# ScalarE empties more banks of the gate recurrence, and one load of y is spread over output products

## The chip, the cores and the metric

The kernel runs on one core of a Trainium2 chip. The metric is the device time of one execution in microseconds (us), as the median of several runs. Times inside an execution come from one profiled execution, read by the hardware profiler; its span is counted from the first to the last instruction. TensorE (PE) multiplies matrices, VectorE (DVE) does elementwise work and scans, ScalarE (ACT) applies functions and copies, GpSimd (POOL) takes some elementwise work, and SyncE (SP) issues the DMA transfers.

## What the kernel computes

Two layers of a diffusion backbone over 1024 latent tokens and 256 context tokens, width 1024, all in float32. Both layers begin with an RMSNorm whose result is shifted and scaled by vectors made from a conditioning input ("modulation"), and end with a gated residual add. Layer 0 has two branches beside each other. Branch A is a gated linear recurrence (RG-LRU): eight heads of 128 channels, a short convolution, two sigmoid gates, and a scan in both directions. Branch B is windowed attention with 16 heads. Layer 1 is another linear recurrence, in chunks (HGRN2). Cut to what the change touches:

```
u      = rmsnorm(h) * w * (1 + scale) + shift        # shift, scale, gate from silu(c) @ ada_w + ada_b
xa, ga, gb = u @ w_in[...]                            # branch A's input, the gates of A and of B
r, i   = sigmoid(conv(xa) @ wa + ba), sigmoid(conv(xa) @ wx + bx)
a      = exp(-8 * r * softplus(-lam));  b = sqrt(1 - a*a) * i * conv(xa)
ya     = scan(a, b) forward + scan(a, b) backward
h      = h + gate * (concat(ya * silu(ga), yb * silu(gb)) @ w_out)      # silu(g) = g * sigmoid(g)
```

## The kernel before, in words

Channels lie on the 128 partitions and tokens on the free axis; the 1280 tokens are three chunks, 0 and 1 of 512 latent tokens and 2 of the 256 context tokens. A float32 product is made of three products of a faster format, from a high and a low half of each operand, so one tile of 512 columns is 3 x 8 matmuls into one bank of PSUM. The weights' halves are made on the chip: `load_w` (L83) loads a block, ScalarE casts it (L93), GpSimd or VectorE takes the difference (L94).

The loop of branch A (L402 to L475) runs over j = 0 to 7, one head each. In iteration j TensorE makes: the gate product of branch A (three chunks, L417 to L422: ScalarE writes the sigmoid from the bank into `sga`, VectorE multiplies it by the bank, which empties the bank); the projection X of the next iteration (copied out by ScalarE, L398); the recurrence's two gates R and I in both directions (twelve products, L436); for j >= 2 the gate product of branch B (three chunks, L466 to L472, into `sgb`, in the same manner, stored in DRAM at L473); and one group of modulation vectors (L163), whose result goes through a ScalarE copy (L166) and a transpose (L174) into a bank that VectorE adds a bias to (L176, `ada_fin`) in the next iteration. ScalarE, GpSimd and VectorE make the recurrence's coefficients between (L437 to L447), VectorE scans (L449 to L456), adds the directions (L460, L461), multiplies them into `sga` (L462, L463), and `sga` is stored (L464).

Banks of PSUM in this stage: four with the tag "mm" for the products, three "gate" for R and I, and one "ada" that the product and the transpose of modulation share. In SBUF, `sga` and `sgb` share one tag of two buffers, so a new one can be written only when the store of an earlier one has landed.

The order of the instructions on each engine is fixed when the kernel is built. In this loop a planner makes it: it takes, engine by engine, what is ready by its own estimates, the earliest in program order first. `tc.high_priority(offset=n)` puts instructions as if they stood n instructions earlier in the program; PRI_E is 100, PRI_W 300. At run time every engine works through its list in order.

After attention, the second half of the output projection (`out_B`, L771) adds branch B's share: `load_yB` (L786) loads y of a chunk in eight pieces `yr` (three buffers), ScalarE casts each to the high half and GpSimd or VectorE makes the low half (L690 to L693). `acc` of each chunk holds the residual and branch A's share, loaded from DRAM (L774); for each of eight blocks m TensorE makes the product of a chunk into one of two banks "mmo", and VectorE adds it to `acc` (L780), ScalarE and VectorE form the sum of squares for the next norm. The first call takes the chunks 2 and 0, the second chunk 1.

Of the kernel before, what the change touches and what calls it, by code (L numbers as in the profile page):

```python
# [11 lines left out]
F32 = mybir.dt.float32  # L12
F32R = mybir.dt.float32r
U8 = mybir.dt.uint8
AF = mybir.ActivationFunctionType
ALU = mybir.AluOpType
# [33 lines left out]
def backbone_kernel(ctx: ExitStack, tc: tile.TileContext, a: dict, out):  # L50
# [82 lines left out]
    def drain(*gens):  # L133
        for g in gens:
            for _ in g:
                pass
# [15 lines left out]
    mods = ctile([128, 2, 6, 4, 2], "mods")  # L152
# [16 lines left out]
    def ada_mod(wpool, psp, l, g, bufs=NADA):  # L169
        ada_fin(psp, ada_mm(wpool, psp, l, g, bufs), l, g)  # L170

    def ada_fin(psp, row, l, g):
        pc = psp.tile([128, 512], F32, tag="ada", name="ps_c", bufs=1)
        PE.transpose(pc[:, :128], row, ident)  # L174
        with tc.high_priority(offset=PRI_E):
            V.tensor_tensor(out=mods[:, l, g], in0=pc[:, :128].rearrange("p (b x) -> p b x", x=32)[:, :, 0:2],  # L176
                            in1=adab[:, l, g].unsqueeze(2).to_broadcast([128, 4, 2]), op=ALU.add)
            if g < 4:
                V.scalar_tensor_tensor(out=amul[:, l, 2 * g:2 * g + 2], in0=mods[:, l, g, 2:4], scalar=1.0,
                                       in1=normw[:, l * 8 + 2 * g:l * 8 + 2 * g + 2].unsqueeze(2)  # L180
                                       .to_broadcast([128, 2, 2]), op0=ALU.add, op1=ALU.mult)
# [110 lines left out]
    def gemm_block(w, c, psp, tag="mm", bufs=4):  # L292
        n = CHUNKS[c][1]
        ps = psp.tile([128, 512], F32, tag=tag, name="mm", bufs=bufs)
        mm3(ps[:, :n], gemm_terms(w, c))
        return ps[:, :n]
# [105 lines left out]
    for j in range(8):  # L402
        X = X_next
        gw = load_w(a["rgw"][j], 512, "gw", rg, bufs=(1, 1))
        uc = rg.tile([128, W], F32, tag="uc", name="uc")
        V.tensor_scalar(out=uc, in0=X[:, 0:W], scalar1=convw[:, j * 4:j * 4 + 1],
                        scalar2=convb[:, j:j + 1], op0=ALU.mult, op1=ALU.add)
        for k in range(1, 4):
            V.scalar_tensor_tensor(out=uc, in0=X[:, k:k + W], scalar=convw[:, j * 4 + k:j * 4 + k + 1],
                                   in1=uc, op0=ALU.mult, op1=ALU.add)  # L410
        uh = rg.tile([128, W], F32R, tag="uh", name="uh")
        ul = rg.tile([128, W], F32R, tag="ul", name="ul")
        V.tensor_copy(uh, uc)
        V.tensor_tensor(out=ul, in0=uc, in1=uh.bitcast(F32), op=ALU.subtract)
        sga = rg.tile([128, T], F32, tag="sga", name="sga", bufs=2)
        w = load_w(a["w0"][8 + j]) if j else w_first[1]
        for c in (2, 0, 1):  # L417
            o, n = CHUNKS[c]
            ps = gemm_block(w, c, psA) if j else ps_first[1, c]
            with tc.high_priority(offset=PRI_E):  # L420
                S.activation(sga[:, o:o + n], ps, AF.Sigmoid)
                V.tensor_tensor(out=sga[:, o:o + n], in0=sga[:, o:o + n], in1=ps, op=ALU.mult)  # L422
        if j < 7:
            X_next = x_proj(j + 1)
        if j:
            ada_fin(psA, row, *ada_lg)
        R, I, A, M = ([rg.tile([128, W], F32, tag=t_, name=t_, bufs=2) for _ in range(2)] for t_ in "RIAM")

        for d in range(2):
            for g_, dst in ((1, R[d]), (0, I[d])):  # L430
                m = (d * 2 + g_) * 128
                for o, n in ((0, 512), (512, 512), (1024, 260)):
                    ps = psA.tile([128, 512], F32, tag="gate", name="gate", bufs=3)
                    mm3(ps[:, :n], [(gw[0][:, m:m + 128], gw[1][:, m:m + 128],
                                     uh[:, o:o + n], ul[:, o:o + n])])
                    S.activation(dst[:, o:o + n], ps[:, :n], AF.Sigmoid, bias=rgb[:, g_, d, j:j + 1])  # L436
            last = S.activation(M[d], R[d], AF.Tanh, scale=sneg[:, d, j:j + 1]).ins  # L437
            G.tensor_tensor(out=I[d], in0=I[d], in1=uc, op=ALU.mult)
        with tc.issue_after(last), tc.high_priority(offset=0):
            for d in range(2):  # L440
                S.activation(A[d], R[d], AF.Exp, scale=spos[:, d, j:j + 1])
        for d in range(2):
            S.activation(R[d], A[d], AF.Square)
            V.scalar_tensor_tensor(out=R[d], in0=R[d], scalar=1.0, in1=M[d], op0=ALU.add, op1=ALU.mult)
        for d in range(2):
            S.activation(R[d], R[d], AF.Sqrt, bias=tiny_c)
            V.tensor_tensor(out=I[d], in0=I[d], in1=R[d], op=ALU.mult)  # L447
            if d == 0:
                V.tensor_tensor_scan(out=M[d][:, CTX0:W], data0=A[d][:, CTX0:W], data1=I[d][:, CTX0:W],  # L449
                                     initial=0.0, op0=ALU.mult, op1=ALU.add)  # L450
                V.tensor_tensor_scan(out=M[d][:, 0:NL], data0=A[d][:, 0:NL], data1=I[d][:, 0:NL],
                                     initial=M[d][:, W - 1:W], op0=ALU.mult, op1=ALU.add)
            else:
                V.tensor_tensor_scan(out=M[d][:, CTX0:W][:, ::-1], data0=A[d][:, CTX0:W][:, ::-1],
                                     data1=I[d][:, CTX0:W][:, ::-1], initial=0.0, op0=ALU.mult, op1=ALU.add)
                V.tensor_tensor_scan(out=M[d][:, 0:NL][:, ::-1], data0=A[d][:, 0:NL][:, ::-1],  # L456
                                     data1=I[d][:, 0:NL][:, ::-1], initial=M[d][:, CTX0:CTX0 + 1],
                                     op0=ALU.mult, op1=ALU.add)
        yf, yb_ = M
        V.tensor_tensor(out=yf[:, 0:NL], in0=yf[:, 0:NL], in1=yb_[:, 0:NL], op=ALU.add)  # L460
        V.tensor_tensor(out=yf[:, CTX0:W], in0=yf[:, CTX0:W], in1=yb_[:, CTX0:W], op=ALU.add)  # L461
        V.tensor_tensor(out=sga[:, 0:NL], in0=sga[:, 0:NL], in1=yf[:, 0:NL], op=ALU.mult)  # L462
        V.tensor_tensor(out=sga[:, NL:T], in0=sga[:, NL:T], in1=yf[:, CTX0:W], op=ALU.mult)  # L463
        SY.dma_start(ya_d[j], sga)  # L464
        if j >= 8 - NGB:
            w = load_w(a["w0"][18 + NGB + j])  # L466
            sg = rg.tile([128, T], F32, tag="sga", name="sgb", bufs=2)
            for c, (o, n) in enumerate(CHUNKS):
                ps = gemm_block(w, c, psA)
                with tc.high_priority(offset=PRI_E):  # L470
                    S.activation(sg[:, o:o + n], ps, AF.Sigmoid)
                    V.tensor_tensor(out=sg[:, o:o + n], in0=sg[:, o:o + n], in1=ps, op=ALU.mult)  # L472
            SY.dma_start(gb_d[(j + NGB - 8) // 2][:, j % 2], sg)  # L473
        ada_lg = (0, 4 + j) if j < 2 else (1, j - 2)
        row = ada_mm(rg, psA, *ada_lg)  # L475
# [213 lines left out]
    def split_y(yp, src, n, hi, lo, k):  # L689
        yr = yp.tile([128, n], F32, tag="yr", name="yr", bufs=3, padded_shape=[128, 512])  # L690
        SY.dma_start(yr, src)
        S.copy(hi[:, k], yr)
        (V if k % 2 else G).tensor_tensor(out=lo[:, k], in0=yr, in1=hi[:, k].bitcast(F32), op=ALU.subtract)  # L693
# [74 lines left out]
    hp0, hp0_st = open_pool("hp0")  # L768
    acc, n1ss = {}, {}

    def out_B(cs, yB, npool, psp, tag, bufs):  # L771
        for c in cs:
            acc[c] = npool.tile([128, 8, CHUNKS[c][1]], F32, tag=f"acc{c}", name=f"acc{c}")
            SY.dma_start(acc[c], hA_d[c])  # L774
            n1ss[c] = npool.tile([128, CHUNKS[c][1]], F32, tag=f"n1ss{c}", name="n1ss")
        for m in range(8):
            w = load_w(a["wo0"][8 + m], split=cs == (1,))
            for c in cs:
                ps, gt = out_half(w, m, yB[c], c, psp, tag, bufs)
                V.scalar_tensor_tensor(out=acc[c][:, m], in0=ps, scalar=gt, in1=acc[c][:, m],  # L780
                                       op0=ALU.mult, op1=ALU.add)
                if c < 2:
                    SY.dma_start(h1_d[:, m, c * 512:c * 512 + 512], acc[c][:, m])
                sumsq(npool, n1ss[c], acc[c][:, m], m)

    def load_yB(c):  # L786
        yB[c] = new_y(c)
        for k in range(8):
            split_y(yrp, yb_d[k // 2][c][:, k % 2], CHUNKS[c][1], *yB[c], k)

    yB = {}
    load_yB(2)
    load_yB(0)
    load_yB(1)
    out_B((2, 0), yB, hp0, psB, "mmo", 2)
    psB_st.close()
    psC, psC_st = open_pool("psC", space=PSUM)
    hp, hp_st = open_pool("hp", side="right")
# [425 lines left out]
```

## Time and profile before

| | |
|---|---|
| median of 3 runs | 1988.04 us (1984.24 to 1995.71) |
| the profiled execution | 1988.59 us |
| its span | 1986.7 us |
| TensorE busy | 1886.1 us (95%), mean granted clock 0.984 |
| VectorE, ScalarE, GpSimd busy | 1146.0, 956.1, 475.1 us |
| DMA | 207.53 MB |

Busy is the time in which an engine worked on at least one instruction; it is not on its own what bounds the kernel. The granted clock is the share of TensorE's full clock that the chip allowed. In the rows further down, L12 is line 12 of the kernel, "a<-b,c" is the written tile and the ones read, and the bracket at the end of a row gives the idle time of the engine before the instruction and what ended it.

### The profile page before, as it was taken

The numbers are of one execution on the slowest core, as the hardware profiler recorded it, in microseconds if no ns is written. First come the engines' busy times: TensorE is split into PE (matmuls) and PEld (weight loads), VectorE is DVE, ScalarE is ACT, GpSimd is POOL, SyncE is SP. The second block draws the span as 40 slices with busy tenths as digits, with TensorE's granted clock in tenths as the row PEclk, the third lists the DMA queues.
The fourth block names the chain that finished last, engine by engine and source line by source line (L and its number), as shares of the span: only waits on it lengthen the run. The fifth ranks groups of instructions, "written<-read, shape, count | busy, mean of one in ns | idle before, by whom it ended". The sixth has DMA issues, their size and how long they took to land. (4 is left out here: it accounts for less than half of the span.)

```text
span 1986.7 us, 36590 instructions
## 1 busy us (share of the span) xinstructions
PE 1886.1 (95%) x15228; PEld 1605.0 (81%) x15228; DVE 1146.0 (58%) x1920; ACT 956.1 (48%) x1766; POOL 475.1 (24%) x309
## 2 busy tenths in 40 slices
PE   6989999999999999999989999999999999998987
PEld 5878888889888787887768889898888779777676
DVE  3766555564465556556534756564746664565656
ACT  4478666682156578556532443434324433343332
POOL 0133332320111024213232222121103212221342
PEclk9999999999999999999999999999999999999998
DMA  8222333323633336435453421111101101110643
GB/s 315 90 97 90 109 106 102 106 91 121 201 99 114 113 123 191 133 120 165 144 171 137 127 68 33 33 57 41 55 33 44 54 26 51 33 52 30 251 141 113
DMA packets 89461, 207.53 MB, mean 104 GB/s; under 512 B 9808, under 2 KB 38224, under 8 KB 88272
## 3 DMA queue, kind: packets, MB, share of 16 engines
q1 hardware_dynamic: 89296, 205.20, 31.5%
q8 instruction: 119, 1.95, 0.4%
q14 instruction: 46, 0.38, 0.1%
HBM read 155.36 MB, written 49.81 MB: 103 GB/s over the span
## 5 line engine op out<-in xcount | busy, mean ns | idle before, releaser
L94 POOL TENSOR_TENSOR w_lo<-w_raw,w_hi 128x1024 fp32r<-128x1024 f32 (+2 forms) x137 | 323.3, 2363 | 1086.7 <-ACT w_hi L93 1008.4
L103 PE MATMUL mm<-u_hi,w_hi 128*128 128x512 f32 (+1 forms) x1456 | 548.0, 376 | 6.7 <-DVE sga L422 3.6
L103 PE MATMUL mm<-u_lo,w_hi 128*128 128x512 f32 (+1 forms) x1456 | 527.6, 362 | 4.7 <-DVE u_lo L250 4.7
L103 PE MATMUL mm<-u_hi,w_lo 128*128 128x512 f32 (+1 forms) x1456 | 527.5, 362 | 0.0
L103 PEld LDWEIGHTS mm<-u_hi,w_hi 128*128 128x128 f32 x1456 | 276.6, 190 | 54.6 <-issue 9.1
L103 PEld LDWEIGHTS mm<-u_hi,w_lo 128*128 128x128 f32 x1456 | 276.0, 190 | 43.4
L103 PEld LDWEIGHTS mm<-u_lo,w_hi 128*128 128x128 f32 x1456 | 276.9, 190 | 41.7 <-DVE u_lo L250 6.6
L93 ACT CAST w_hi<-w_raw 128x1024 fp32r<-128x1024 f32 (+2 forms) x163 | 141.6, 884 | 218.8 <-PE mm L103 95.6
L103 PE MATMUL mmo<-y_hi,w_hi 128*128 128x512 f32 (+1 forms) x384 | 146.5, 381 | 7.6 <-DVE acc L780 7.6
L599 DVE CUSTOM_DVE_ANT_0 p<-s_ps,maskA 128x640 f32<-128x640 f32 (+2 forms) x160 | 110.3, 713 | 58.8 <-PE s_ps L594 58.7
L610 ACT ACTIVATE p<-p,nm 128x640 f32<-128x640 f32 (+2 forms) x160 | 118.7, 743 | 42.8 <-DVE nm L606 39.0
L103 PE MATMUL mmo<-y_hi,w_lo 128*128 128x512 f32 (+1 forms) x384 | 138.0, 359 | 0.0
L103 PE MATMUL mmo<-y_lo,w_hi 128*128 128x512 f32 (+1 forms) x384 | 137.6, 358 | 0.0
L627 ACT COPY pt<-t 128x512 f32<-128x512 f32 x168 | 94.8, 582 | 81.3 <-PE t L624 80.9
L103 PE MATMUL mm_v<-w_hi,u_hi 128*128 128x256 f32 x400 | 115.3, 288 | 0.0
L103 PE MATMUL mm_v<-w_lo,u_hi 128*128 128x256 f32 x400 | 113.1, 283 | 0.0
L103 PE MATMUL mm_v<-w_hi,u_lo 128*128 128x256 f32 x400 | 113.1, 283 | 0.0
L624 PE MATMUL t<-ident,p 128*128 128x128 f32 x672 | 98.4, 273 | 4.7 <-ACT pt L627 2.9
L103 PE MATMUL mm_o<-yT,w_hi 128*128 128x256 f32 (+1 forms) x384 | 93.2, 338 | 8.3 <-DMA yT<-y_d 3.2
L945 DVE TENSOR_TENSOR KK<-KK,tot 128x1280 f32<-128x1280 f32 x48 | 74.1, 1544 | 40.3 <-PE lv L931 25.2
L624 PEld LDWEIGHTS t<-ident,p 128*128 128x128 f32 x672 | 80.5, 141 | 19.7 <-ACT pt L627 4.9
L103 PEld LDWEIGHTS mmo<-y_hi,w_hi 128*128 128x128 f32 x384 | 73.8, 192 | 22.8 <-DVE acc L780 8.3
(219 smaller groups left out, 3492.3 us busy)
## 6 DMA issues: line engine op xcount, KB each, us to landing
w_raw<-w_in SPq DMA_DIRECT2D x66, 512.0 KB, 3.7
ada<-ada_w_in SPq DMA_DIRECT2D x48, 512.0 KB, 6.3
w_raw<-wo_in SPq DMA_DIRECT2D x32, 512.0 KB, 3.7
qt<-q_d SPq DMA_DIRECT2D x20, 512.0 KB, 4.8
y_d<-yhl SPq DMA_DIRECT2D x14, 512.0 KB, 2.7
yT<-y_d SPq DMA_DIRECT2D x14, 512.0 KB, 10.9
w_raw<-wo1m_in SPq DMA_DIRECT2D x12, 512.0 KB, 3.8
xin<-hT_in SPq DMA_DIRECT2D x5, 1024.0 KB, 9.0
```

Source lines behind the costliest of these rows:

```text
L93: S.copy(hi[:, o:m], raw[:, o:m])
L94: eng.tensor_tensor(out=lo[:, o:m], in0=raw[:, o:m], in1=hi[:, o:m].bitcast(F32), op=ALU.subtract)
L103: ins = PE.matmul(ps, l, r, start=(first and i == 0), stop=(last and i == n - 1))
L599: V.tensor_tensor_reduce(out=p[:, :nk], in0=s_ps[:, c0[x]:c0[x] + nk], in1=self.msks[x], scale=1.0, scalar=NEG, op0=ALU.add, op1=ALU.max, ...
L610: S.activation(p, p, AF.Exp, scale=0.125, bias=nm[:, x:x + 1], accum_out=dn[:, x:x + 1])
L624: PE.transpose(pt[:, h], self.P[h][:, o:o + 128], ident)
L627: S.copy(ptc, pt)
L945: V.tensor_tensor(out=kv_, in0=kv_, in1=custom(tot, 1, [[2, nb // 2], [nb - 1, 2], [0, hb]]), op=ALU.mult)
```

## The change

Three edits. In `ada_fin`, for the seven calls inside the loop, ScalarE copies the eight columns of the bank that count into an SBUF tile `m_sb`, and VectorE adds the bias from there. In branch B's gates, ScalarE copies each bank into an SBUF tile `gr` (two buffers); the sigmoid and the multiply read `gr` instead of the bank, and both lose the priority PRI_E, which the copy has now. In the output projection `load_yB` becomes a generator that pauses after each of its eight pieces; the chunks 2 and 0 are loaded ahead as before, and the eight pieces of chunk 1 are placed one by one into the blocks m of the first `out_B`, behind the load of that block's weights. So they stand after the loads of `acc2` and `acc0` in the program. (`drain` runs generators to their end.)

```diff
-    def ada_fin(psp, row, l, g):
+    def ada_fin(psp, row, l, g, pool=None):
         pc = psp.tile([128, 512], F32, tag="ada", name="ps_c", bufs=1)
         PE.transpose(pc[:, :128], row, ident)
         with tc.high_priority(offset=PRI_E):
-            V.tensor_tensor(out=mods[:, l, g], in0=pc[:, :128].rearrange("p (b x) -> p b x", x=32)[:, :, 0:2],
+            mc = pc[:, :128].rearrange("p (b x) -> p b x", x=32)[:, :, 0:2]
+            if pool:
+                m_sb = pool.tile([128, 4, 2], F32, tag="m_sb", name="m_sb", bufs=2)
+                S.copy(m_sb, mc)
+                mc = m_sb
+            V.tensor_tensor(out=mods[:, l, g], in0=mc,
                             in1=adab[:, l, g].unsqueeze(2).to_broadcast([128, 4, 2]), op=ALU.add)
...
         if j:
-            ada_fin(psA, row, *ada_lg)
+            ada_fin(psA, row, *ada_lg, rg)
...
                 ps = gemm_block(w, c, psA)
+                gr = rg.tile([128, n], F32, tag="gr", name="gr", bufs=2, padded_shape=[128, 512])
                 with tc.high_priority(offset=PRI_E):
-                    S.activation(sg[:, o:o + n], ps, AF.Sigmoid)
-                    V.tensor_tensor(out=sg[:, o:o + n], in0=sg[:, o:o + n], in1=ps, op=ALU.mult)
+                    S.copy(gr, ps)
+                S.activation(sg[:, o:o + n], gr, AF.Sigmoid)
+                V.tensor_tensor(out=sg[:, o:o + n], in0=sg[:, o:o + n], in1=gr, op=ALU.mult)
...
-    def out_B(cs, yB, npool, psp, tag, bufs):
+    def out_B(cs, yB, npool, psp, tag, bufs, beside=None):
...
             w = load_w(a["wo0"][8 + m], split=cs == (1,))
+            if beside:
+                next(beside)
...
             split_y(yrp, yb_d[k // 2][c][:, k % 2], CHUNKS[c][1], *yB[c], k)
+            yield
 
     yB = {}
-    load_yB(2)
-    load_yB(0)
-    load_yB(1)
-    out_B((2, 0), yB, hp0, psB, "mmo", 2)
+    drain(load_yB(2), load_yB(0))
+    out_B((2, 0), yB, hp0, psB, "mmo", 2, load_yB(1))
```

## Rows read from the trace of the kernel before

**Rows 1.** The page, part 1: busy us (share of the span) and instructions.
```profile
PE 1886.1 (95%) x15228; PEld 1605.0 (81%) x15228; DVE 1146.0 (58%) x1920; ACT 956.1 (48%) x1766; POOL 475.1 (24%) x309
```

**Rows 2.** Waits of PE: us in total, times, longest.
```profile
PE mmo L103 <- DVE acc L780: 7.6, 2, 7.0
...
PE ps_m L163 <- DVE mods L176: 5.1, 1, 5.1
...
PE mm L103 <- DVE sga L422: 3.6, 4, 0.9
```

**Rows 3.** Stretches: length, busy PE, PEld, DVE, ACT, POOL, PEclk, DMA share, GB/s.
```profile
137.50:146.40 8.90, 3.85 (x13) 2.80 (x12) 5.18 (x6) 2.81 (x5) 2.22 (x1) 0.81 0.34 108
220.00:235.00 15.00, 14.10 (x64) 11.37 (x64) 2.73 (x6) 3.68 (x7) 4.72 (x2) 1.00 0.26 88
787.80:796.80 9.00, 8.99 (x48) 7.10 (x49) 6.46 (x14) 7.02 (x17) 3.35 (x4) 0.81 0.84 245
1031.00:1045.00 14.00, 6.44 (x29) 5.78 (x28) 3.41 (x6) 4.76 (x8) 4.90 (x3) 0.63 0.96 359
```

**Rows 4.** Timeline of DVE in iteration 1: start, us, instruction.
```profile
137.50 2.50 DVE L461 TENSOR_TENSOR M<-M 128x256 f32<-128x256 f32 x1
...
142.53 0.15 DVE L176 TENSOR_TENSOR mods<-ps_c,c_adabT 128x8 f32<-128x8 f32 x1
```

**Rows 5.** Timeline of ACT between iterations 2 and 3.
```profile
209.78 1.28 ACT L421 ACT_TABLE_LOAD   x1 [0.29 <-DMA gb_d<-sgb]
211.08 0.38 ACT L421 ACTIVATE sga<-mm 128x256 f32<-128x256 f32 x1
211.36 0.26 ACT L166 COPY adar<-ps_m 128x128 f32<-128x128 f32 x1
```

**Rows 6.** Timeline of DVE in the same stretch.
```profile
200.78 1.55 DVE L409 SCALAR_TENSOR_TENSOR uc<-X,convw,uc 128x1284 f32<-128x1284 f32 x1
...
204.72 1.01 DVE L472 TENSOR_TENSOR sgb<-sgb,mm 128x512 f32<-128x512 f32 x2
...
217.88 0.39 DVE L461 TENSOR_TENSOR M<-M 128x256 f32<-128x256 f32 x1
...
219.67 1.21 DVE L462 TENSOR_TENSOR sga<-sga,M 128x1024 f32<-128x1024 f32 x1
220.80 1.60 DVE L422 TENSOR_TENSOR sga<-sga,mm 128x256 f32<-128x256 f32 x3
```

**Rows 7.** Line 464, the store of sga: time from issue to landing.
```profile
DMA to landing us min/median/max: 2.9/2.9/3.5
```

**Rows 8.** Timeline of PE at one of the waits named L422.
```profile
221.26 0.50 PE L103 MATMUL mm<-u_hi,w_hi 128*128 128x512 f32 x1 [0.90 <-DVE sga L422]
```

**Rows 9.** Timeline of PE in attention, an idle time of middling length.
```profile
787.80 0.40 PE L593 MATMUL s_ps<-khh,qt 128*128 128x256 f32 x1 [2.81 <-DVE mx L599]
```

**Rows 10.** Timeline of ACT in iteration 7.
```profile
425.93 1.14 ACT L93 CAST w_hi<-w_raw 128x512 fp32r<-128x512 f32 x2 [4.66 <-PE mm L103]
426.98 0.59 ACT L421 ACTIVATE sga<-mm 128x512 f32<-128x512 f32 x1
427.47 1.63 ACT L436 ACTIVATE R<-gate,rgb 128x512 f32<-128x512 f32 x3
```

**Rows 11.** Timeline of DVE in the same stretch.
```profile
427.15 1.21 DVE L462 TENSOR_TENSOR sga<-sga,M 128x1024 f32<-128x1024 f32 x1
```

**Rows 12.** Timeline of PE in the same stretch.
```profile
428.24 0.46 PE L103 MATMUL gate<-uh,w_hi 128*128 128x512 f32 x1
```

**Rows 13.** Timeline of SP, its issues at the start of branch B's output products.
```profile
1028.06 1.57 SPq L691 DMA_DIRECT2D yr<-yb_d  x3
1029.68 0.42 SPq L774 DMA_DIRECT2D acc<-hA_d  x1
```

**Rows 14.** Line 774, the loads of acc: time from issue to landing.
```profile
DMA to landing us min/median/max: 8.0/10.2/11.6
```

**Rows 15.** Timeline of PE in the same stretch.
```profile
1044.34 0.50 PE L103 MATMUL mmo<-y_hi,w_hi 128*128 128x512 f32 x1 [0.58 <-DVE acc L780]
```

## The prediction

> **What bounds the kernel now.** I read the page first: TensorE is busy 1886.1 us, 95% of the span [rows 1]. So the change can only pay where TensorE stands idle, and cost only where it makes TensorE wait. I then read TensorE's waits by what ended them [rows 2] and looked for the lines of the diff. Three rows name them: 5.1 us once, modulation's matmul behind the add that empties the bank (L176); 3.6 us in four waits, a product behind branch A's gate multiply (L422); 7.6 us in two, branch B's output product behind the accumulation L780. That is 16.3 us of waits. The third view, busy time by stretches, shows the granted clock around each [rows 3]: 0.81 over the 8.90 us that hold the first wait and 0.63 over the 14 us that hold the last, against 1.00 over the stretch that holds one of the four small ones. Taking those means as time at the chip's two levels (2.4 and 1.2 GHz), a mean of 0.81 over 8.90 us is 0.19 x 8.90 = 1.7 us of full-speed work lost, 0.63 over 14 us is 5.2 us. All the change can win is about 16.3 + 1.7 + 5.2 = 23 us. Everything else is a question of order: PE, ScalarE and VectorE are in-order queues here, and what is queued behind a late instruction is late too.
>
> **Part 1, modulation through ScalarE.** Seven small copies on ScalarE are added, and the add L176 reads SBUF. What it removes: in iteration 1 the bank stays taken until VectorE has worked off its queue, from L461 at 137.50 to L176 at 142.53 [rows 4]; PE waits 5.1 for it [rows 2]. ScalarE has a free slot then (2.81 busy in 8.90, [rows 3]), and the copy costs as little as the copy of the same bank at 211.36, 0.26 us [rows 5]. So the bank is free before PE needs it. I take 5.05 us and the 1.7 us of clock: −6.7. Bounds: 0 (the copy queued behind gate activations in ScalarE whose gates are behind this very matmul) and −6.8. The other six adds made no PE wait, since the row counts one, so six more copies are hidden in ScalarE's free time. What is late next there: the gates' own chain, which runs at PE's pace.
>
> **Part 2, branch B's gates through ScalarE.** In each of six iterations three copies are added on ScalarE (bounds: 0.26 for 128 wide to 0.59 for a sigmoid of 512, [rows 5, 10]). About 18 x 0.5 = 9 us, hidden: PE waits for ScalarE in none of the rows that name these banks [rows 2]. The banks come free without VectorE. But the sigmoid and the multiply lose their 100 instructions of priority. The sigmoids now rank below the same iteration's exponentials, squares and roots, and the multiplies below its scans and gate products, since those stand earlier in the program. Before, two multiplies ran at 204.72 for 1.01 us, ahead of the scans [rows 6]; now I put those of chunks 1 and 2 behind L462, the last of that chain, at 219.67 + 1.21 = 220.88 [rows 6].
>
> Who waits for that? Not a bank, but a buffer. The gates of A (sga) and of B (sgb) share one tag with two buffers. The row at 209.78 shows branch A's next sigmoid held 0.29 us by the store of sgb, and it ran at 211.08 [rows 5]. If sgb is stored only after the scans, the next sga must wait for whichever store lands first: sga's own, issued when L462 ends. Without the two multiplies L462 ends at 220.88 − 1.01 = 219.87; the store lands 2.9 us (median, [rows 7]) after that, at 222.8; then a sigmoid of 0.38 [rows 5] and a multiply of about 0.4 on VectorE (the smallest of three that took 1.60, [rows 6]): 223.6, and I allow 0.2 for the hand-overs: 223.8. PE needs that bank; before it resumed at 221.26 [rows 8]. Each of the four waits of 0.90 grows by about 2.6, to 3.5 us. What of the clock? After 0.90 idle it stayed at 1.00 [rows 3, 8]; after 2.81 idle [rows 9] the next 9.00 us had a mean of 0.81 [rows 3], 1.7 us lost again. 3.5 is above 2.81, so I add 1.7: 4 x (2.6 + 1.7) = +17.2. Bounds: −3.6 (the multiplies still stand before the scans, and all four waits vanish, [rows 2]) and +17.2.
>
> **Iteration 7** is another place. There sga's sigmoids of chunks 2 and 0 come ahead of two casts (1.14), chunk 1's sigmoid and the R gates' activations (1.63 for three, so 0.55 the first) in ScalarE's queue [rows 10]. If they wait for the store of iteration 6 (L462 ends at 427.15 + 1.21 = 428.36 [rows 11], less 1.0, plus 2.9: 430.3), the first gate bank comes free at 430.3 + 0.38 + 0.59 + 1.14 + 0.59 + 0.55 = 433.5. PE starts the fourth of those gate products at 428.24 [rows 12] and has three banks for them: it stops for about 5.2, plus 1.7 of clock: +6.9. Bounds 0 and +6.9.
>
> **A price on SBUF inputs.** The multiply and the modulation add read two SBUF operands now instead of one. L461, which does so, took 2.50 us at 137.50 with one GpSimd instruction running beside it [rows 3, 4], and 0.39 at 217.88 [rows 6]. The Trainium skill ("SBUF — State Buffer", section "Who interferes with whom") says that a VectorE instruction with two SBUF inputs contends with a GpSimd instruction that reads SBUF, and that one of the two then blocks; the two rows agree. GpSimd is busy 4.72 of 15 us in the loop [rows 3], about a third, so of 18 multiplies some six could last 2 us longer. They push PE only where they stand ahead of L462 or L422; I price that at 0 to +4 in all (a sum of 2005 instead of 2001), and take 0, since in the likeliest order they stand behind the chain that PE waits for.
>
> **Part 3, the last chunk of y.** Eight loads, casts and differences move from before the output products of chunks 2 and 0 into them, one per m. Before, three yr loads are issued at 1028.06 and the load of acc2 behind them at 1029.68 [rows 13]; it lands 8.0 us later at the least [rows 14], at 1037.7. PE waits 7.0 and 0.6 for the sums that read it and acc0 [rows 2, 15], partly at half clock. With acc ahead of yr in the program, acc2 could be issued 2 to 3 us earlier, without the loads beside it that now fill the queues (0.96 of the DMA share, [rows 3]): 3.5 to 6.6 us off the start of the next product, 1044.34 now. But loads of yr are ready as early as before, and the order of SyncE's queue is made by a planner that takes what is ready; with it unchanged the gain is 0 to 1. I take −3.5 as the middle; bounds 0 and −12.8 (7.0 + 0.6 + 5.2 of clock). Moving it I cost at nothing: in the 14 us of that stretch ScalarE was busy 4.76, VectorE 3.41 and GpSimd 4.90 with some of these very casts in it [rows 3], and chunk 1 of y is read only after all products of chunks 2 and 0. If that cover were gone, PE would wait there for one last cast and difference, at most a GpSimd instruction (4.90 / 3 = 1.6) and a cast: 2 to 3 us.
>
> **Sum** −6.7 + 17.2 + 6.9 − 3.5 = +13.9 on the profiled 1988.59 (span 1986.7 and 1.9 around it), 2002.5; on the median 1988.04, 2001.9. I say 2001. Of this case the own range is 1987 (four waits without loss of clock, +10.4, iteration 7 at 0, part 3 at −5) to 2016 (parts 1 and 3 at 0, SBUF inputs +4).
>
> **Rivals.**
> Late buffer (the forecast, slower): 2001, decided by whether L472's last multiply stands behind L462 in VectorE's queue. For it: plain priority and a queue with no gap from conv to scan. Against: the planner fills VectorE while it waits for the roots, and part of the convolution of iteration j+1, which ranks lower still, ran there before (L409 at 200.78, [rows 6]).
> Gates in time (faster): the multiplies take those places, the stores go out before the scans end, as now. Then −6.7, 0 to −3.6, and 0 to −12.8 at the output: middle −6.7 − 1.8 − 3.5 = −12.0, so 1976.5; all of it 1966. For it: two multiplies before scans are already there [rows 6].
> Bank wait that only moves: ScalarE's copy waits behind activations that wait for the gates, in iteration 1 and again in the others, so part 1 brings 0 and SyncE's order is kept: 1988 with the gates in time, 1985 to 1990. It counts as no change.
> Contended inputs: gates in time, but up to 4 us of longer VectorE work ahead of L462, so −12.0 + 4: 1980.5.
>
> **How the numbers follow.** Late buffer 0.60, gates in time 0.24, moved waits 0.10, contended inputs 0.06. No change means within 0.5%, 9.9 us, about what a measurement of this kernel can tell: 1978 to 1998. Late buffer ends above 1998 in four of five cases (0.48) and else within; gates in time ends below 1978 in 0.20 of its 0.24; the contended case in 0.03 of 0.06. So faster 0.23, same 0.29, slower 0.48. The range: 1971 leaves out the best cases of gates in time (0.08), 2012 the worst of late buffer (0.12).
>
> **What would show it.** Right: VectorE's order puts L472 after L462; SyncE issues the ya_d store before the gb_d store; L421's first sigmoid waits for a DMA ya_d<-sga; PE waits "mm L103 <- DVE sga L422" of 3 us or more, with a granted clock under 1.00 after them; the ps_m wait gone. Wrong: those waits stay near 0.9 or vanish, with the gb_d store issued before the scans; or the ps_m wait now ends on ScalarE's copy; or acc2 is still issued behind three yr loads.

## The result

The changed kernel is slower: 2009.94 us median (2007.37 to 2010.16, 4 runs) against 1988.51 us (1984.24 to 1995.71, 4 runs); the ratio is 1.010 with a 95% interval of [1.0079, 1.0122]. The profiled execution took 2010.16 with a span of 2008.4, so 21.7 us more than the span before.

First view, the page of the changed kernel, part 1 (answers to [rows 1]). TensorE's busy time rose by 12.8 us with the same 15228 matmuls, at a mean granted clock of 0.974 against 0.984: that is clock, not work.

```profile
PE 1898.9 (95%) x15228; PEld 1615.5 (80%) x15228; DVE 1152.4 (57%) x1920; ACT 947.4 (47%) x1780; POOL 473.2 (24%) x309
```

Second, TensorE's waits in the changed kernel (answers to [rows 2]; us in total, times, longest). The lines have moved: L427 is the old L422, L789 the old L780, L441 the old L436.

```profile
PE mm L103 <- DVE sga L427: 12.2, 4, 3.1
...
PE gate L103 <- ACT R L441: 4.9, 2, 4.7
PE mmo L103 <- DVE acc L789: 4.6, 2, 4.1
PE mm_v L103 <- ACT v_sb L503: 4.1, 1, 4.1
```

The four waits on sga's multiply went from 3.6 to 12.2; a wait of 4.7 in iteration 7 and one of 4.1 behind the loop are new; the wait on acc fell from 7.6 to 4.6; the ps_m wait of 5.1 is gone from the list.

Third, the stretches of the changed kernel (answers to [rows 3], same columns).

```profile
140.00:149.00 9.00, 7.44 (x96) 6.13 (x95) 2.34 (x4) 7.96 (x12) 4.83 (x3) 1.00 0.66 217
212.70:227.70 15.00, 11.98 (x61) 10.08 (x60) 3.76 (x9) 3.16 (x6) 2.40 (x1) 1.00 0.34 123
...
266.00:281.00 15.00, 11.96 (x64) 10.19 (x63) 4.63 (x11) 3.16 (x6) 2.40 (x1) 1.00 0.31 122
...
326.00:341.00 15.00, 14.91 (x54) 12.04 (x55) 1.41 (x3) 3.55 (x7) 2.44 (x2) 0.80 0.14 39
383.00:392.00 9.00, 9.00 (x33) 7.28 (x34) 1.36 (x2) 2.23 (x4) 2.37 (x1) 0.81 0.18 59
439.84:452.00 12.16, 12.16 (x48) 9.99 (x49) 0.25 (x2) 10.11 (x15) 4.86 (x3) 0.81 0.15 43
478.00:488.00 10.00, 9.02 (x64) 9.02 (x65) 0.17 (x1) 1.95 (x6) 0.00 (x0) 0.83 0.95 331
1055.18:1065.00 9.82, 9.24 (x44) 8.27 (x45) 2.17 (x4) 2.46 (x5) 1.29 (x1) 0.83 0.72 269
```

The clock is at 1.00 behind iteration 1 now, stays there behind the first two of the four waits, and is lost behind the third and fourth of the four waits, in iteration 7 and behind the loop. The last row begins where TensorE resumes at the output: 0.83 over 9.82 us. In the kernel before, over the 5.49 us in which TensorE worked between its two waits there, it was 0.50:

```profile
1038.27:1043.76 5.49, 5.49 (x24) 5.19 (x24) 0.83 (x1) 1.53 (x3) 2.16 (x2) 0.50 0.96 392
```

Fourth, the mechanism in one iteration. VectorE's timeline of the changed kernel, the same stretch as [rows 6]:

```profile
212.48 1.22 DVE L467 TENSOR_TENSOR sga<-sga,M 128x1024 f32<-128x1024 f32 x1
213.62 1.02 DVE L479 TENSOR_TENSOR sgb<-sgb,gr 128x512 f32<-128x512 f32 x2
...
217.18 1.18 DVE L427 TENSOR_TENSOR sga<-sga,mm 128x256 f32<-128x256 f32 x2 [2.52 <-ACT sga L426]
```

SyncE's issues there:

```profile
213.72 0.33 SPq L469 DMA_DIRECT2D ya_d<-sga  x1
214.66 0.33 SPq L480 DMA_DIRECT2D gb_d<-sgb  x1
```

And ScalarE (answers to [rows 5]):

```profile
198.76 1.37 ACT L451 ACTIVATE R<-R,tiny 128x1284 f32<-128x1284 f32 x1 [0.75 <-DVE R L449]
...
202.38 0.94 ACT L478 ACTIVATE sgb<-gr 128x512 f32<-128x512 f32 x2
...
216.76 0.87 ACT L426 ACTIVATE sga<-mm 128x256 f32<-128x256 f32 x2 [13.29 <-DMA ya_d<-sga]
```

Read them in the order of time. The sigmoids of chunks 1 and 2 of branch B stand behind the square roots (202.38). Their multiplies stand behind L467 (213.62), the last of the scans' chain. So the store of sga goes out before that of sgb, and branch A's next sigmoid waits 13.29 us for it, until 216.76. TensorE has no free bank and stands still for 3.02 us here:

```profile
217.66 0.50 PE L103 MATMUL mm<-u_hi,w_hi 128*128 128x512 f32 x1 [3.02 <-DVE sga L427]
```

### The profile page after: what moved, and what is told of

Read it like the earlier page. It is cut to its first block, busy times and chain, and to the rows that moved or that the text cites. A ratio compares the mean times of both kernels' runs of the same rounds, so it can differ in the third digit from the quotient of the medians.

```text
span 2008.4 us, 36584 instructions
## 1 busy us (share of the span) xinstructions
PE 1898.9 (95%) x15228; PEld 1615.5 (80%) x15228; DVE 1152.4 (57%) x1920; ACT 947.4 (47%) x1780; POOL 473.2 (24%) x309
## 5 line engine op out<-in xcount | busy, mean ns | idle before, releaser
L103 PE MATMUL mm<-u_hi,w_hi 128*128 128x512 f32 (+1 forms) x1456 | 551.6, 379 | 15.2 <-DVE sga L427 12.2
```

The costliest lines, as they stand in the source:

```text
L103: ins = PE.matmul(ps, l, r, start=(first and i == 0), stop=(last and i == n - 1))
```

## The experiments

Each was timed in five rounds with runs of the kernel before on the same chip; the ratio is to those.

**Branch B's gates alone.** The kernel before with this edit only:

```diff
                 with tc.high_priority(offset=PRI_E):
-                    S.activation(sg[:, o:o + n], ps, AF.Sigmoid)
-                    V.tensor_tensor(out=sg[:, o:o + n], in0=sg[:, o:o + n], in1=ps, op=ALU.mult)
+                    S.copy(gr, ps)
+                S.activation(sg[:, o:o + n], gr, AF.Sigmoid)
+                V.tensor_tensor(out=sg[:, o:o + n], in0=sg[:, o:o + n], in1=gr, op=ALU.mult)
```

> The kernel before with branch B's gates alone changed (copy to gr; sigmoid and multiply without priority). Theory, late buffer: the whole loss is made by this part, and the two other parts win about 5 us at iteration 1 and about 3 to 4 us at branch B's output products, so alone it costs more than the whole change: 2018 us (2013 to 2023), with the four waits on sga's multiply at 3.0 us, a wait of 4 to 5 us in iteration 7, and the ps_m wait of about 5 us still there. Rival, the loss comes from the parts together (ScalarE loaded by all the added copies): less than the whole change's 2010.

2020.09 us, ratio 1.015 [1.0134, 1.0166]: about 10 us slower than the whole change. TensorE's waits, this kernel:

```profile
PE mm L103 <- DVE sga L422: 12.4, 4, 3.1
...
PE mmo L103 <- DVE acc L782: 7.3, 2, 6.7
PE ps_m L163 <- DVE mods L176: 5.0, 1, 5.0
...
PE gate L103 <- ACT R L436: 4.9, 2, 4.6
PE mm_v L103 <- ACT v_sb L498: 4.3, 1, 4.3
```

The three new waits are all here, and the two old ones that the other parts remove are back. The whole loss belongs to this part.

**Without it.** The changed kernel with branch B's gates as before, the diff above reversed.

> The changed kernel with branch B's gates as before (modulation through ScalarE and the spread load of y kept). Theory: both parts are gains, 1988.5 - 5.5 - 3.5 = 1979.5 us (1975 to 1984); the four waits on sga's multiply at 0.9 us each as before, no ps_m wait of 5 us, the wait on acc at about 4. Rival, that ScalarE's copies or two SBUF inputs cost something by themselves: 1986 or more.

1981.78 us, ratio 0.9953 [0.9941, 0.9965]. Its waits have the four of 0.9 and, less than the 4 that I expected, 2.6 on acc:

```profile
PE mm L103 <- DVE sga L427: 3.6, 4, 0.9
...
PE mmo L103 <- DVE acc L787: 2.6, 2, 2.0
```

**Modulation's copy alone.** As the run before, with chunk 1 of y loaded ahead again:

```diff
-    drain(load_yB(2), load_yB(0))
-    out_B((2, 0), yB, hp0, psB, "mmo", 2, load_yB(1))
+    drain(load_yB(2), load_yB(0), load_yB(1))
+    out_B((2, 0), yB, hp0, psB, "mmo", 2)
```

> The kernel before with modulation's copy through ScalarE alone. Theory: the ps_m wait of 5.1 us turns into one of about 1.6 on ScalarE's gate activation, and the clock stays at 1.00 behind it: 5 to 5.5 us less, ratio 0.9975 (0.9955 to 0.999); the output's wait on acc stays at 6 to 7. So of the 9 us that this part and the load of y win together, the load has 3 to 5. Rival: this part brings nothing by itself, ratio 1.000 or more.

1984.65 us, ratio 0.9971 [0.9961, 0.9980]; the wait on acc is 6.6 in two. So modulation brings about 6 us and the load of y, by the difference of the two runs, about 3 to 4 (on different chips, and the intervals touch).

**Priority given back to sigmoid and multiply**, the copies kept:

```diff
                 with tc.high_priority(offset=PRI_E):
                     S.copy(gr, ps)
-                S.activation(sg[:, o:o + n], gr, AF.Sigmoid)
-                V.tensor_tensor(out=sg[:, o:o + n], in0=sg[:, o:o + n], in1=gr, op=ALU.mult)
+                    S.activation(sg[:, o:o + n], gr, AF.Sigmoid)
+                    V.tensor_tensor(out=sg[:, o:o + n], in0=sg[:, o:o + n], in1=gr, op=ALU.mult)
```

> The changed kernel, with sigmoid and multiply of branch B's gates inside the priority of 100 again; the copies into gr and both SBUF inputs stay. Theory, late buffer: the multiplies stand before the long scans, gb_d is stored before ya_d, sga no longer waits for a ya_d store, the four waits fall to 0.5 to 1.5 us each: 1979 us (1974 to 1985). Rival, the added ScalarE copies and the contention of two SBUF inputs with GpSimd are what costs: 1995 to 2010.

2001.2 us, ratio 1.0049 [1.0031, 1.0067]. A miss, outside my range by 16 us. The four waits are longer than with the change:

```profile
PE mm L103 <- DVE sga L427: 14.6, 4, 3.7
```

But the buffer is not what they wait for. ScalarE, this kernel:

```profile
203.19 1.28 ACT L478 ACT_TABLE_LOAD   x1
204.49 0.42 ACT L478 ACTIVATE sgb<-gr 128x256 f32<-128x256 f32 x1
204.92 1.28 ACT L451 ACT_TABLE_LOAD   x1
206.22 1.37 ACT L451 ACTIVATE R<-R,tiny 128x1284 f32<-128x1284 f32 x1
...
209.25 1.28 ACT L426 ACT_TABLE_LOAD   x1 [0.57 <-DMA gb_d<-sgb]
210.55 0.87 ACT L426 ACTIVATE sga<-mm 128x256 f32<-128x256 f32 x2
```

VectorE:

```profile
212.24 2.35 DVE L461 TENSOR_TENSOR_SCAN M<-A,M,I 128x1024 f32<-128x1024 f32 x1
...
214.83 3.41 DVE L465 TENSOR_TENSOR M<-M 128x1024 f32<-128x1024 f32 x1
```

GpSimd:

```profile
214.53 2.62 POOL L94 TENSOR_TENSOR w_lo<-w_raw,w_hi 128x1024 fp32r<-128x1024 f32 x1 [2.88 <-ACT w_hi L93]
```

Sga's sigmoid runs at 210.55, in good time; its multiply waits in VectorE's queue behind a late chain. Two things make it late. The sigmoid of chunk 2 now splits the two square roots, with two more table loads of 1.28 us (in all L478 has 18 loads instead of 12, L451 16 instead of 10). And L465, two SBUF operands, ran beside a GpSimd subtraction: 3.41 us here, 2.31 in the mean of eight, 1.21 in the change. L465 read two SBUF operands before the change too (the old L460, 1.21); what is new is that it falls beside the subtraction. The Trainium skill ("SBUF — State Buffer", section "Who interferes with whom") says that such a VectorE instruction contends with a GpSimd instruction that reads SBUF, and these two rows agree. The next run takes both causes away at once (12 and 10 loads, L465 at 1.21 again), so their shares are not told apart.

**Only the multiply given its priority back**, the sigmoid left where the change has it:

```diff
                 S.activation(sg[:, o:o + n], gr, AF.Sigmoid)
-                V.tensor_tensor(out=sg[:, o:o + n], in0=sg[:, o:o + n], in1=gr, op=ALU.mult)
+                with tc.high_priority(offset=PRI_E):
+                    V.tensor_tensor(out=sg[:, o:o + n], in0=sg[:, o:o + n], in1=gr, op=ALU.mult)
```

> The changed kernel with the multiply of branch B's gates alone given back its priority of 100; the sigmoid stays without, the copies and the two SBUF inputs stay. It asks why giving priority back to both brought little. Theory: there the sigmoid of chunk 2 split the two square roots on ScalarE (two more loads of a table in each iteration) and made the scans late; with the sigmoids behind the roots, as in the change, and only the multiplies early, the table loads are those of the change, gb_d is stored before ya_d, and TensorE's four waits on sga's multiply are 0.5 to 1.7 us each, without iteration 7's 4.7: 1984 us against 1990 before (1979 to 1989). Rival, the copies and the two SBUF inputs cost by themselves: waits of 3 us or more, 1996 or more.

1977.99 us, ratio 0.9940 [0.9922, 0.9957], 1 us below my range. Its waits and its issues on SyncE:

```profile
PE mm L103 <- DVE sga L427: 1.6, 4, 0.4
```

```profile
210.11 0.33 SPq L481 DMA_DIRECT2D gb_d<-sgb  x1
215.29 0.33 SPq L469 DMA_DIRECT2D ya_d<-sga  x1
```

Sgb is stored first again, and the waits are shorter than before the change. The copies, the two SBUF operands and ScalarE's added work are all still there, so none of them was the price by itself. The place of one multiply was: 0.016 of the ratio, some 32 us, lies between this kernel and the change.

**A third buffer, late multiplies kept.** `bufs=2` to `bufs=3` for the tag that sga and sgb share; to make room, three buffers instead of four for modulation's weights:

```diff
-NADA = 4
+NADA = 3
...
-        sga = rg.tile([128, T], F32, tag="sga", name="sga", bufs=2)
+        sga = rg.tile([128, T], F32, tag="sga", name="sga", bufs=3)
...
-            sg = rg.tile([128, T], F32, tag="sga", name="sgb", bufs=2)
+            sg = rg.tile([128, T], F32, tag="sga", name="sgb", bufs=3)
```

> The changed kernel with three buffers instead of two for the tag that sga and sgb share (and, to make room, three instead of four buffers for modulation's weights); sigmoid and multiply of branch B still without priority, so the late multiplies stay. Theory, late buffer: it is the buffer and not the lateness that TensorE pays for, so the waits on sga's multiply fall from 3.0 to about 1 us each, the sigmoid of sga no longer waits for a DMA ya_d<-sga in iterations 3 to 6, and iteration 7's wait goes: 1985 us (1978 to 1992). Rival, late multiplies cost by their place in VectorE's queue: waits stay near 3 us, 2005 to 2010.

1995.83 us, ratio 1.0030 [1.0019, 1.0042], 4 us above my range, though no wait on sga's multiply is left at all. Its waits show why:

```profile
PE ps_m L163 <- DMA ada<-ada_w_in: 8.2, 7, 3.0
...
PE mm_v L103 <- ACT v_sb L503: 3.5, 1, 3.5
```

The room that I took cost 8.2. So once more, taking it elsewhere:

```diff
-                gr = rg.tile([128, n], F32, tag="gr", name="gr", bufs=2, padded_shape=[128, 512])
+                gr = rg.tile([128, n], F32, tag="gr2" if c == 2 else "gr", name="gr", bufs=1)
```

> The changed kernel with three buffers for the tag of sga and sgb, modulation's four weight buffers kept; room is made by one gr buffer of 512 columns and one of 256 instead of two of 512. Late multiplies stay. Theory, the buffer: waits on sga's multiply gone as with three buffers before, and the 8 us of waits on modulation's weights, which I put down to the buffer taken from them there, gone too; the wait at the first copy of v after the loop (3.5 us and its lower clock) stays: 1985 us against 1990 before (1980 to 1990). Rival, those waits belong to the three buffers of sga: 1994 to 1998 again.

1982.66 us, ratio 0.9959 [0.9946, 0.9972]. The waits on modulation's weights are gone, those on sga's multiply too; of the new ones only that on v stays, 4.2 us. The multiplies are as late as in the change; VectorE's row in the stretch of the first of the four waits:

```profile
213.81 2.56 DVE L479 TENSOR_TENSOR sgb<-sgb,gr 128x512 f32<-128x512 f32 x1
```

So in the four waits TensorE paid for the buffer, not for the lateness. The row is also the collision that the prediction set at nothing: this multiply takes 0.68 in the change, and four of the twelve wide ones take 2.56 here, this one beside a GpSimd subtraction from 212.61 to 215.82. TensorE waits for none of them.

**Branch A's gates earlier**, branch B's as before:

```diff
-            with tc.high_priority(offset=PRI_E):
+            with tc.high_priority(offset=PRI_W):
                 S.activation(sga[:, o:o + n], ps, AF.Sigmoid)
                 V.tensor_tensor(out=sga[:, o:o + n], in0=sga[:, o:o + n], in1=ps, op=ALU.mult)
```

> The changed kernel with branch B's gates as before, and branch A's sigmoid and multiply at a priority of 300 instead of 100, so that the multiplies stand ahead of the products of the scans. Theory: the four waits of 0.9 us on sga's multiply, which came from its place behind the scans, vanish: 3.6 us less than without that, ratio to before 0.9935 (0.992 to 0.996). Rival: the scans' own results come later by the same multiplies, and the time is that without it, 0.9955, or worse.

1977.79 us, ratio 0.9933 [0.9921, 0.9946]; no wait on sga is left. It was a second way to the same gain, so I put both together, this diff and that of the multiply alone, on the changed kernel.

> The changed kernel with the multiply of branch B's gates at priority 100 again, and branch A's sigmoid and multiply at 300. Theory: what is left of the four waits on sga's multiply (0.4 us each) and the 1.6 us at iteration 1 go or shrink as they did with the priority of 300 alone; 1 to 4 us less than with the multiply alone: ratio to before 0.9925 (0.991 to 0.9945), the fastest of all. Rival: sga's sigmoid is still held by the store of sgb, which lands late here, so the higher priority finds nothing to put earlier: 0.994.

1980.51 us, ratio 0.9958 [0.9946, 0.9971]: a miss, not the fastest. The waits:

```profile
PE mm L103 <- DVE X L397: 2.0, 1, 2.0
...
PE mm L103 <- DVE sga L427: 1.3, 3, 0.5
```

The rival's mechanism holds: sga's sigmoid is still held by the store of sgb (ScalarE stood idle for it 41.5 us in five times, 42.7 with the multiply alone), so there is nothing to put earlier. The wait of 2.0 is the first of the same four: it bears the name of a clearing of X that ended at 216.28, but sga's multiply ended only 0.03 us earlier. Why it is longer than the other three was not settled. Then the same with the third buffer as well (`bufs=3` for sga and sgb, and gr as in the second of the two diffs there):

> The same with three buffers for the tag of sga and sgb (gr in one buffer of 512 and one of 256 columns). Theory: with the buffer free nothing holds sga's sigmoid, no wait on sga's multiply is left, and the wait at the first copy of v after the loop does not come back, since the multiplies stand before the last scan: ratio 0.9925 (0.9905 to 0.9945). Rival: one gr buffer of 512 makes ScalarE's second copy wait for the first multiply and holds a bank: 0.995 or more.

1975.28 us, ratio 0.9932 [0.9917, 0.9947], no wait on sga and none on v. Three kernels (this one, the higher priority of branch A, the multiply's priority) have the lowest ratios, 13 to 14 us of median under the kernel before. Their intervals overlap with each other and, at their ends, with those of the three at 0.995 to 0.996: which is the fastest is not settled.

## Why the prediction was right

**The mechanism** was the forecast's: the order of L479 behind L467, ya_d before gb_d, L426 waiting for a DMA ya_d<-sga (65.3 us in five times in the changed kernel), four waits of 3.0 to 3.1. Only the sign of a granted clock under 1.00 after them came in two of the four. From the end of the scans' chain to TensorE's resuming the forecast had 3.9 us (219.87 to 223.8); measured are 4.0 (213.70 to 217.66). The third buffer (with a smaller gr to make room) and the multiply's priority, each alone, take the four waits' loss away. Forecast 2001, measured 2009.94: inside the range of 1971 to 2012, but near its upper end. The time rose by 21.4 us where 13 were forecast.

**Its terms**, from the profiled pair:

Iteration 1, −6.7: 5.1 went to 1.6, and the clock's 1.7 came back, so −5.2. What is late next was named too kindly. TensorE meets a wait on ScalarE: the gate's activation stands behind one that waits for VectorE.

```profile
140.88 1.36 ACT L442 ACTIVATE M<-R,sneg 128x1284 f32<-128x1284 f32 x1 [1.61 <-DVE M L465]
142.16 1.04 ACT L441 ACTIVATE I<-gate,rgb 128x512 f32<-128x512 f32 x2
```

The four waits, +17.2: 12.2 − 3.6 = 8.6 of waiting (forecast 10.4), and of clock 0.20 x 15 + 0.19 x 9 = 4.7 (forecast 6.8): +13.3. The first two waits were as long as the others, 3.0 us, but the clock stayed at 1.00 behind them. (The forecast's own figures put TensorE's resuming at 223.75, so 2.5 later, not 2.6; in the sum that is 0.4.)

Iteration 7, +6.9: 4.7, and, over the time in which TensorE worked, 0.19 x 12.16 = 2.3 of clock: +7.0.

The load of y, −3.5: 7.6 − 4.6 = 3.0 of waiting. Of clock the prediction saw 5.2 to win, 0.37 x 14, but for more than half of those 14 us TensorE stood idle, and a low clock costs nothing there. While it worked it lost 0.50 x 5.49 = 2.7 before and 0.17 x 9.82 = 1.7 after, so 1.0 was won: −4.0. The bound of −12.8 and the 23 us that the change could win at most are too large by the same 2.5. The order is the forecast's: SyncE issues both acc loads ahead of yr.

```profile
1046.57 2.08 SPq L781 DMA_DIRECT2D acc<-hA_d  x2
1048.70 0.92 SPq L698 DMA_DIRECT2D yr<-yb_d  x2
```

TensorE at its wait, the changed kernel and then the one before:

```profile
1055.18 0.39 PE L103 MATMUL mmo<-y_hi,w_hi 128*128 128x256 f32 x1 [4.07 <-DVE acc L789]
```

```profile
1038.27 0.58 PE L103 MATMUL mmo<-y_hi,w_hi 128*128 128x256 f32 x1 [6.98 <-DVE acc L780]
```

TensorE stops at 1055.18 − 4.07 = 1051.11, 4.5 us behind the first acc issue; before it stopped at 1031.29, 1.6 behind [rows 13]. So the load went out 2.9 earlier, and as it still takes 8.0 to land, 2.9 is what was won. The prediction did not say how 2 to 3 us of earlier issue become 3.5 to 6.6; that its 3.5 lies near 4.0 is in part luck.

SBUF inputs, 0: the twelve wide multiplies took 681 ns in the mean, 682 before. Right in the change. The price came in the kernel with three buffers and all four weight buffers (2.56 us above), where it cost TensorE nothing; in the run with both priorities L465 paid one, but its operands were not the change's doing.

**What the forecast left out** is a wait behind the loop. ScalarE's first copy of v, changed kernel:

```profile
478.56 1.20 ACT L503 COPY v_sb<-mm_v 128x256 f32<-128x256 f32 x4 [11.49 <-DMA ya_d<-sga]
```

V's tile lies in space that the loop gives back, and that space is free only when iteration 7's sga is stored, issued at 475.51. TensorE waits 4.1, with 0.17 x 10 = 1.7 of clock behind it: +5.8. In the kernel before, the first copy ran at 453.62, and the store went out at 464.00: v's space did not hang on it there. I read this from the releaser; that the two buffers changed roles is inferred and was not tested by itself. It stays with a third buffer, and is gone when the multiply is early.

**The sum** is −5.2 + 13.3 + 7.0 + 5.8 − 4.0 = +16.9, of 21.7. The start of the matmul with the same number in both traces shows where the rest lies: matmul 3480, after the loop, starts 20.3 us later than before, number 6000, ahead of branch B's output products, 20.1, number 6600, behind their start, 16.0, and the last 21.7. Up to there the terms agree with the trace within 1 us, and the output's gain is 4.1. So some 5.7 come in code that the change doesn't touch. The two stretches, before and after:

```profile
1062.00:1986.70 924.70, 874.03 (x8635) 755.58 (x8634) 555.00 (x727) 344.91 (x659) 212.93 (x111) 0.98 0.21 70
```

```profile
1078.50:2008.40 929.90, 880.54 (x8633) 760.70 (x8632) 554.55 (x726) 344.73 (x659) 212.80 (x111) 0.97 0.21 70
```

5.2 us more there, 6.5 more of busy TensorE, at 0.97 instead of 0.98. The kernel with branch A's gates earlier has the same:

```profile
1046.00:1976.30 930.30, 879.37 (x8635) 760.36 (x8633) 554.82 (x727) 344.64 (x659) 212.41 (x111) 0.97 0.21 69
```

Yet the one with the multiply's priority does not (12.7 us ahead at number 6600, 12.9 at the last). So this part moves from kernel to kernel. It also moves with one and the same kernel: the kernel before ran from 1984.48 us (mean granted clock 0.984) to 1992.84 (0.979) in one series, and its profiled execution is one at 0.984. These 5.7 us are therefore not shown to be a cost of the edit; what decides them is open.

**Why my sum came out low:** by the wait behind the loop (5.8), which hangs on the same late store and which I did not follow past iteration 7, by iteration 1, which won 1.5 less, and by the clock of layer 1, open as said. That the forecast came as near as it did is in part luck: the four waits cost 3.9 less than forecast, which made up for part of what was left out.

## What to carry to other kernels

When an instruction loses priority, ask which buffer its result sits in and who takes that buffer next; a tag that two uses share ties one engine's order to another's stores. An edit that frees a bank sooner can hold a buffer longer: price both. A low clock costs only where TensorE works: take it over the working time, not over a stretch with a wait in it. And where a priority is given back, look at each instruction by itself: the multiply's was worth some 32 us (0.016 of the ratio), and the sigmoid's took 22 of them away again (0.011).

## What the runs showed that I had not expected

Of four waits of 3.0 us in the changed kernel, two were followed by a granted clock of 1.00 and two by 0.80 and 0.81, the rows of the third view; in the kernel with branch B's gates alone it was again the first two and the last two. The four waits of 3.7 in the kernel with both priorities were all followed by a lower one. In layer 1 the same wait of 1.1 us (PE at L969, L977 after the change, for VectorE) was followed by full clock before the change and by a lower one after it; the two stretches of 15 us, before and after:

```profile
1438.00:1453.00 15.00, 12.36 (x71) 9.84 (x70) 13.47 (x25) 2.35 (x5) 2.36 (x1) 1.00 0.12 35
```

```profile
1455.50:1470.50 15.00, 12.41 (x64) 10.13 (x63) 12.72 (x22) 2.26 (x5) 2.36 (x1) 0.89 0.13 35
```

So the length of one wait alone did not decide the clock, and a sum that adds 1.7 us for each wait above some length, as mine did, is a guess in each single place.
